# Attention on one Trainium2 core: the keys of the second head pair are loaded on ScalarE's DMA queue

## The chip, the cores and the metric

The kernel runs on one core of a Trainium2 chip. The metric is the device time in microseconds (us) of one launch; lower is better. The engines of the core are TensorE (PE, with its weight loads listed as PEld), VectorE (DVE), ScalarE (ACT), GpSimd (POOL) and SyncE (SP); transfers between the device memory and the core's SBUF are carried by 16 DMA engines and are issued here from two queues, SP's (q1 in the profile) and ScalarE's (q10).

## The reference

Softmax attention without a mask, in float32, for 8 batches of 8 heads, 512 positions and 64 columns:

```python
scale = 1.0 / np.sqrt(q.shape[-1])
scores = np.einsum('bhqd,bhkd->bhqk', q, k) * scale
scores = scores - scores.max(axis=-1, keepdims=True)
attn = np.exp(scores)
attn = attn / attn.sum(axis=-1, keepdims=True)
return np.einsum('bhqk,bhkd->bhqd', attn, v).astype(np.float32)
```

q, k, v and the output are 8 x 8 x 512 x 64 values each, 8.39 MB apiece.

## The kernel before, in words

**Tiling.** The 64 heads are taken two at a time: 32 pairs, g = 0 to 31. For each pair there are three loads of 256 KB (k, q and v, two heads of 512 x 64 float32 on 128 partitions). POOL casts them to float16 (L494, L504), PE transposes k and q (L535), DVE copies the transposes out of PSUM (L548, for pair 1 in two halves at L542), and PE then forms the scores (L575), 128 keys by 512 queries for each head and block of keys. Two such blocks are one group of 128 x 1024 scores, and there are 128 groups (the last one in two halves). For 112 of them ACT takes the exponential (L579, L777); for the other 16 DVE does it by arithmetic on the bits (L599, L616 to L639). PE multiplies by the values (L680), a column of ones beside v gives the sums, DVE takes reciprocals and scales (L645, L650), and a store goes out for each head.

**Order.** Nothing is scheduled at run time. The class `Plan` simulates the kernel with fixed durations and due times and writes out one list of steps; the body issues them in that order under `tc.manual_schedule()`, so each engine runs its instructions in a fixed order and only waits for semaphores. The plan has no notion of which queue a load is on: it has one stream of transfers.

**The start, where the change is.** `first_loads()` (L718) issues pair 0's keys in two halves on ScalarE's queue (L722) and pair 0's queries in two halves on SP's (L723). Then a loop calls `load(g, name)` for pair 1's keys ("k1" below), pair 1's queries ("q1"), k2, q2, v0, k3, q3, k4, q4, k5, q5, v1 and so on, all on SP's queue at L488. The loads' completion is told on eight semaphores taken in turn, so that SP issues a load only when the one eight places before it has landed: q4's issue waits for k1's landing, k5's for q1's, and so on; SP's later issues stand behind.

`first_pair()` (L729) handles pair 0 by itself: ACT loads its activation table (L743), then casts a part of q0 (L743), and of the second halves (L745, L746); DVE and POOL cast the rest; PE transposes them (L760, L765), with some matmuls on constants between (L727), and forms pair 0's first three groups of scores (L770), whose exponentials ACT takes at L777. The fourth group of pair 0 and all later ones are at L575 and L579.

**Pair 1.** POOL casts k1 whole (L504). q1 is cast in two halves at once, by DVE (L502) and by POOL (L503), where POOL's half stands behind its cast of k1. PE transposes k1 first and then q1 (L535, eight 128 x 128 blocks), DVE copies k1's half and then q1's (L542), and the first scores of pair 1 follow at L575. Behind these casts POOL has k2, q2 and v0.

Of the kernel before, what the change touches and what calls it, by code (L numbers as in the profile page):

```python
# [407 lines left out]
def kernel(  # L408
# [7 lines left out]
    nc = tc.nc  # L416
# [50 lines left out]
    def source(src, g):  # L467
        b, h = g // ppb, 2 * (g % ppb)
        return src[b, h : h + 2].rearrange("h (p i) d -> p h i d", i=NI)

    def load_tile(g, name):
        t = lpool.tile(
            [P, 2, NI, D],
            FP32,
            tag=f"{name}32",
            name=f"{name}32_{g}",
            bufs=7,
        )
        raw.setdefault(g, {})[name] = t
        return t  # L480

    def load(g, names):
        if g >= NP:
            return
        for name in names:
            src = {"q": q, "k": k, "v": v}[name]
            t = load_tile(g, name)
            nc.sync.dma_start(out=t[:, :, :, :], in_=source(src, g))  # L488

    def cast(g, name):  # L490
        if g >= NP:
# [325 lines left out]
    with tc.manual_schedule():  # L817
        plan = Plan(groups, NP, 3)
        steps = plan.run()
        first_loads()  # L820
        for g, name in plan.first_loads:
            load(g, name)
        make_identity(nc, ident)
        for n in range(NV):
            nc.vector.memset(vps[n][:, :, :, D : D + 1], 1.0)
        first_pair()
        do = {
            "transposes": transposes,
            "scores": scores,
            "values": values,  # L830
            "load": load,
            "store": store,
            "cast": cast_behind,
            "raise": raise_,
            "copy": lambda g, b: copy(g),
            "pass": pass_,
            "last": last_values,
            "finish": finish,
            "rec": lambda u, n, b: reciprocal(u, n),
            "mul": lambda u, n, b: normalise(u, n),  # L840
        }
        for what, *args in steps:
            do[what](*args)
# [30 lines left out]
```

## Time and profile before

| | |
|---|---|
| median of 3 runs | 114.5 us (113.86, 114.7, 114.5) |
| the profiled execution | 114.31 us, of which the span of the instructions is 112.5 us |
| POOL busy | 65.2 us (58%) |
| TensorE's granted clock, mean | 0.999 |
| read from device memory, written to it | 25.17 MB, 8.39 MB |
| DMA queue q1 (SP's), q10 (ScalarE's) | 33.04 MB, 0.52 MB |

The profile is of one execution. A row of the timeline gives the start and the length in us (merged instructions with their count), the engine (with a q where it is the engine's queue that issues something), the line, the operation, out<-in, and in brackets the engine's idle time before it and what ended that. Rows of a line's instructions give the duration in ns as minimum/median/maximum and the start of the first and the last; "DMA to landing" is the time from issue to the completion of a transfer, in us. Rows by windows give, for a stretch of the span, each engine's busy time and the number of its instructions, then the granted TensorE clock, the mean busy share of the 16 DMA engines (it can pass 1, as packets overlap) and the rate in GB/s.

### The profile page before, as it was taken

How to read it: one execution, taken by the hardware profiler on the slowest of the kernel's cores; microseconds unless marked ns; L12 is line 12 of the kernel's file. 1: busy time of each engine (PE TensorE's matmuls, PEld its weight loads, DVE VectorE, ACT ScalarE, POOL GpSimd, SP SyncE). 2: the span in 40 equal slices, each digit the busy share in tenths (PEclk: the TensorE clock that was granted, in tenths of full speed). 3: DMA queues.
4: the chain of work that ended last, by engine and by line, in shares of the span. 5: the costliest groups of instructions: out<-in, count | busy, mean ns of one | idle time of the engine just before them, and what ended most of it. 6: DMA issues, size and time to landing. Idle time of an engine off the chain costs nothing.

```text
span 112.5 us, 4427 instructions
## 1 busy us (share of the span) xinstructions
PE 104.0 (92%) x1731; PEld 71.1 (63%) x1731; DVE 101.3 (90%) x226; ACT 105.6 (94%) x118; POOL 65.2 (58%) x127
## 2 busy tenths in 40 slices
PE   7988889899999998999999999999999999999970
PEld 7654546576775564657677557678667765776560
DVE  1547999999989999999999999999999999999760
ACT  4689999999999999999999999999999999999960
POOL 2166788265478866686847888755868796000000
PEclk9999999999999999999999999999999999999999
DMA  2999999999999999999999999999997976848435
GB/s 90 271 340 354 346 349 349 342 349 348 348 329 331 344 350 347 344 353 325 283 299 376 346 312 363 358 374 353 357 305 229 289 244 212 270 143 268 159 99 184
DMA packets 35349, 33.84 MB, mean 301 GB/s; under 512 B 2560, under 2 KB 35328, under 8 KB 35328
## 3 DMA queue, kind: packets, MB, share of 16 engines
q1 hardware_dynamic: 34752, 33.04, 90.8%
q10 hardware_dynamic: 576, 0.52, 1.4%
q8 instruction: 13, 0.21, 0.8%
q14 instruction: 8, 0.07, 0.2%
HBM read 25.17 MB, written 8.39 MB: 298 GB/s over the span
## 4 chain that ended last, share of the span: by engine, by line
DVE 45%; PE 42%; ACT 7%; issue 2%; DMA 1%
PE o L680 18%; PE st L575 14%; DVE pd L599 10%; DVE tqk L548 8%; DVE ring L650 8%; ACT pt L579 7%; PE tp L535 6%; DVE m L633 4%; DVE pd L639 3%; PE st_0a L727 3%; DVE pe L625 3%; DVE m L616 2%; DVE m L635 2%; DVE rc L645 2%; DMA out_dram<-ring 1%
## 5 line engine op out<-in xcount | busy, mean ns | idle before, releaser
L579 ACT ACTIVATE pt<-st 128x1024 f16<-128x1024 f32 (+1 forms) x110 | 100.3, 1114 | 0.0
L680 PEld LDWEIGHTS <-pt 128*128 128x128 f16 x880 | 38.9, 98 | 12.3 <-issue 10.6
L680 PE MATMUL o<-vp,pt 128*128 128x65 f16 x880 | 46.3, 194 | 0.2
L575 PE MATMUL st<-tqk 64*128 64x512 f16 (+1 forms) x250 | 42.4, 381 | 2.9 <-ACT pt L579 1.7
L504 POOL CAST qkp<-k 128x512 f16<-128x512 f32 x31 | 21.5, 692 | 12.2 <-DMA k<-in_k_dram 5.2
L494 POOL CAST vp<-v 128x512 f16<-128x512 f32 x32 | 21.8, 695 | 7.7 <-DVE rc L645 2.6
L504 POOL CAST qkp<-q 128x512 f16<-128x512 f32 x30 | 21.1, 703 | 6.6 <-DVE rc L645 2.2
L650 DVE TENSOR_TENSOR ring<-o,rc 128x448 f32<-128x448 f32 (+2 forms) x37 | 22.3, 606 | 0.6
L680 PE MATMUL o<-vp,pe 128*128 128x65 f16 x128 | 22.1, 195 | 0.0
L680 PE MATMUL o<-vp,pd 128*128 128x65 f16 x128 | 21.9, 193 | 0.0
L548 DVE COPY tqk<-tp 128x1024 f16<-128x1024 f16 x30 | 20.3, 677 | 0.2 <-PE tp L535 0.2
L535 PE MATMUL tp<-ident,qkp 128*128 128x128 f16 x248 | 19.5, 219 | 0.9 <-DVE ring L650 0.7
L599 DVE TENSOR_SCALAR pd<-st 128x1024 uint16<-128x1024 f32 x16 | 19.5, 1217 | 0.7 <-PE st L575 0.7
L575 PEld LDWEIGHTS <-tqk 64*128 64x128 f16 x250 | 11.7, 93 | 12.3 <-issue 4.8
L535 PEld LDWEIGHTS <-qkp 128*128 128x128 f16 x248 | 14.3, 97 | 7.3 <-issue 4.4
L680 PEld LDWEIGHTS <-pe 128*128 128x128 f16 x128 | 12.5, 97 | 3.8 <-issue 2.9
L680 PEld LDWEIGHTS <-pd 128*128 128x128 f16 x128 | 12.5, 98 | 0.0
L639 DVE TENSOR_TENSOR pd<-pd,m 128x1024 f16<-128x1024 f16 x16 | 10.9, 682 | 0.0
L633 DVE TENSOR_TENSOR m<-m 128x1024 f16<-128x1024 f16 x16 | 10.9, 681 | 0.0
L645 DVE RECIPROCAL rc<-o 128x7 f32<-128x7 f32 (+2 forms) x37 | 7.2, 195 | 1.9 <-PE o L680 1.9
L625 DVE TENSOR_SCALAR pe<-pd 128x1024 uint16<-128x1024 uint16 x16 | 6.8, 425 | 0.0
L635 DVE TENSOR_SCALAR m<-m 128x1024 f16<-128x1024 f16 x16 | 6.5, 409 | 0.0
(50 smaller groups left out, 36.6 us busy)
## 6 DMA issues: line engine op xcount, KB each, us to landing
v<-in_v_dram SPq DMA_DIRECT2D x32, 256.0 KB, 5.8
k<-in_k_dram SPq DMA_DIRECT2D x31, 256.0 KB, 5.9
q<-in_q_dram SPq DMA_DIRECT2D x31, 256.0 KB, 5.9
out_dram<-ring SPq DMA_DIRECT2D x57, 128.0 KB, 3.7
out_dram<-ring SPq DMA_DIRECT2D x2, 256.0 KB, 3.3
k<-in_k_dram ACTq DMA_DIRECT2D x2, 128.0 KB, 2.9
q<-in_q_dram SPq DMA_DIRECT2D x2, 128.0 KB, 2.7
out_dram<-ring ACTq DMA_DIRECT2D x2, 128.0 KB, 2.0
```

What stands on the lines that cost most here:

```text
L494: return nc.gpsimd.tensor_copy(out=vps[g % NV][:, :, :, 0:D], in_=raw[g]["v"][:, :, :, :])
L504: return nc.gpsimd.tensor_copy(out=dst, in_=src[:, :, :, :])
L535: reads[g] = nc.tensor.transpose(tps[g][:, n, i, :], qkp[g][:, n, i, :], ident)
L548: nc.vector.tensor_copy(out=tqk[g][:, :, :], in_=tps.pop(g).rearrange("p n i c -> p n (i c)"))
L575: nc.tensor.matmul(st[:, x, cols], kc, qc[:, cols], start=True, stop=True)
L579: nc.scalar.activation(out=pt[:, :, cols], in_=st[:, :, cols], func=EXP, scale=scale, bias=SHIFT)
L599: nc.vector.tensor_scalar(out=r["pd"][:, :, :], in0=r["st"][:, :, :], scalar1=BITS, scalar2=BIAS, op0=AluOp.mult, op1=AluOp.add,)
L625: ins = nc.vector.tensor_scalar(out=r["pe"][:, :, :], in0=u[:, :, :], scalar1=0x7C00, scalar2=None, op0=AluOp.bitwise_and,)
L633: ins = nc.vector.tensor_tensor(out=m16, in0=m16, in1=m16, op=AluOp.mult)
L639: ins = nc.vector.tensor_tensor(out=u16, in0=u16, in1=m16, op=AluOp.mult)
L650: nc.vector.tensor_tensor(out=ring[:, u % NU : u % NU + n, :], in0=o[:, x : x + n, 0:D], in1=rcs.pop(u)[:, 0:n].broadcast_to([P, n, D]), o ...
L680: nc.tensor.matmul(os[u // 7][:, u % 7, :], part[:, y * P : (y + 1) * P], vps[g % NV][:, h, c, :], start=(n == 0), stop=(n == len(parts) - 1),
```

## The change

One transfer changes queue. The load of pair 1's keys is issued by ScalarE instead of SyncE; it stands behind the two halves of pair 0's keys on ScalarE's queue, and ahead of ScalarE's table load, because `first_loads()` and this loop come before `first_pair()`. Each of SP's later loads moves up by one place. The order of every engine's other instructions is the same, and so are the semaphores that the loads use. All lines behind L488 move down by one.

```diff
         for name in names:
             src = {"q": q, "k": k, "v": v}[name]
             t = load_tile(g, name)
-            nc.sync.dma_start(out=t[:, :, :, :], in_=source(src, g))
+            queue = nc.scalar if (g, name) == (1, "k") else nc.sync
+            queue.dma_start(out=t[:, :, :, :], in_=source(src, g))
```

## The prediction

> **What bounds the kernel now.** I read the page first, for who is busy and what ended last, then the busy time by windows, then the timeline of the first 10 us, where the moved transfer is, then the landings of the transfers around it.
>
> ```profile
> DVE 45%; PE 42%; ACT 7%; issue 2%; DMA 1%
> ...
> L579 ACT ACTIVATE pt<-st 128x1024 f16<-128x1024 f32 (+1 forms) x110 | 100.3, 1114 | 0.0
> ```
>
> The chain that ended last runs through DVE and PE; DMA has 1% of it. But the 110 exponentials of L579 have no idle time before them at all. By windows:
>
> ```profile
> core 0: us, PE busy (x) PEld busy (x) DVE busy (x) ACT busy (x) POOL busy (x), PEclk, DMA share, GB/s
> 0.00:9.43 9.43, 7.76 (x95) 5.68 (x95) 3.60 (x24) 6.40 (x10) 3.58 (x12) 1.00 0.79 247
> 9.43:26.00 16.57, 15.23 (x231) 9.72 (x230) 16.53 (x32) 16.57 (x19) 11.17 (x20) 1.00 1.09 347
> 26.00:50.00 24.00, 22.52 (x377) 15.42 (x376) 23.38 (x47) 24.00 (x27) 17.18 (x37) 1.00 1.08 343
> 50.00:90.00 40.00, 39.63 (x703) 27.38 (x700) 39.59 (x85) 40.00 (x45) 28.85 (x54) 1.00 1.00 327
> ```
>
> From 9.43 to 90 us ACT is busy 80.57 of 80.57 us and DVE 79.50. These two are full, so a delay of the moment at which they become full is paid to the end, and time saved elsewhere is worth nothing unless they become full sooner. The DMA engines are full too (share 1.00 to 1.09), but only POOL waits for them, and POOL has 28.85 busy of 40. So the change is decided in the first 9.43 us:
>
> ```profile
> 0.74 0.89 ACTq L722 DMA_DIRECT2D k<-in_k_dram  x2
> 0.75 0.86 SPq L723 DMA_DIRECT2D q<-in_q_dram  x2
> 1.66 0.43 SPq L488 DMA_DIRECT2D k<-in_k_dram  x1
> 1.67 1.28 ACT L743 ACT_TABLE_LOAD   x1 [1.67 <-PEq L858]
> 2.12 0.47 SPq L488 DMA_DIRECT2D q<-in_q_dram  x1
> ...
> 3.28 0.41 ACT L743 CAST q<-q 128x256 f16<-128x256 f32 x1 [0.33 <-DMA q<-in_q_dram]
> ...
> 4.04 0.42 PE L765 MATMUL st<-ident,q 128*128 128x128 f16 x2
> ...
> 6.13 0.61 POOL L504 CAST qkp<-k 128x512 f16<-128x512 f32 x1 [2.27 <-DMA k<-in_k_dram]
> ...
> 7.01 0.29 DVE L502 CAST qkp<-q 128x256 f16<-128x256 f32 x1
> 7.04 0.52 POOL L503 CAST qkp<-q 128x256 f16<-128x256 f32 x1 [0.29 <-DMA q<-in_q_dram]
> ...
> 7.54 0.62 PE L535 MATMUL tp<-ident,qkp 128*128 128x128 f16 x8
> 7.79 0.61 POOL L504 CAST qkp<-k 128x512 f16<-128x512 f32 x1 [0.22 <-DMA k<-in_k_dram]
> 7.97 0.76 DVE L542 COPY tqk<-tp 128x512 f16<-128x512 f16 x2 [0.67 <-PE tp L535]
> 8.35 1.94 ACT L579 ACTIVATE pt<-st 128x1024 f16<-128x1024 f32 x2
> ...
> 8.54 0.61 POOL L504 CAST qkp<-q 128x512 f16<-128x512 f32 x1
> 8.79 1.03 PE L575 MATMUL st<-tqk 64*128 64x512 f16 x6 [0.63 <-DVE tqk L542]
> 9.43 1.23 DVE L599 TENSOR_SCALAR pd<-st 128x1024 uint16<-128x1024 f32 x1 [0.71 <-PE st L575]
> ```
>
> The reader is to follow pair 1. k1 is cast at 6.13 and q1 at 7.01 to 7.04, each as it lands. Transposes run from 7.54, the two copies from 7.97, the first scores start at 8.79, and DVE's first exponential, which needs the next ones, at 9.43; from there DVE is full. ACT's two exponentials from 8.35 take 1.94 us, some 0.97 each, so the second, the first of pair 1, starts at about 9.3. Nothing between 7.54 and 9.43 waits for more than its predecessor.
>
> **ScalarE's queue.** One more issue stands ahead of the table load. Those on this queue took 0.89 for two, so 0.45 each: the table load goes from 1.67 to about 2.12 and ends at 3.40, not 2.95. The cast behind it waited for q0 until 3.28; it now starts at about 3.42, 0.14 later, and ends at 3.83. PE reads it at 4.04, behind other transposes. That slack of 0.35 (4.04 less 3.28 + 0.41) hides the 0.14: cost nothing. An issue can take longer:
>
> ```profile
> L488 SPq DMA_DIRECT2D k<-in_k_dram x31: 367/368/1184, 1.7 to 76.4; - x31
> ```
>
> At 1.18, the longest, the cast would end 0.87 later than now, and 0.5 would reach PE. That is the upper bound, and it can't be a gain; I take nothing, as the two issues on this very queue are the nearest rows. The last three casts of pair 0 on ACT and DVE wait for transfers already ahead of k1.
>
> **SP's queue.** k1's 0.43 goes, and q1, k2, q2 and so on are issued about 0.47 sooner. That is worth nothing by itself if their landing is not set by the issue, and it isn't: q1 is issued at 2.12 and cast 4.9 us later. q4, the eighth load behind k1, waits for k1's landing, and all later loads stand behind it on SP. With k1 landing 1 us later, six transfers (k2 to k4) are still queued, at some 0.75 each (POOL's casts of k2 and q2 start at 7.79 and 8.54) 4.5 us of work, so the DMA engines do not run dry.
>
> **When k1 lands** is the term that counts. Landings from the issue:
>
> ```profile
> L722 ACTq DMA_DIRECT2D k<-in_k_dram x2: 403/432/460, 0.7 to 1.2; - x2
> DMA to landing us min/median/max: 2.7/2.9/3.2
> ...
> L723 SPq DMA_DIRECT2D q<-in_q_dram x2: 381/399/417, 0.7 to 1.2; - x2
> DMA to landing us min/median/max: 2.5/2.7/2.9
> ...
> L488 SPq DMA_DIRECT2D k<-in_k_dram x1: 427/427/427, 1.7 to 1.7; - x1
> DMA to landing us min/median/max: 4.4/4.4/4.4
> ...
> L488 SPq DMA_DIRECT2D q<-in_q_dram x1: 469/469/469, 2.1 to 2.1; - x1
> DMA to landing us min/median/max: 4.9/4.9/4.9
> ```
>
> k1 lands at 1.66 + 4.4 = 6.1 and q1 at 2.12 + 4.9 = 7.0. On one queue k1 goes first and q1 second. On two, both are issued at about 1.65 and are carried side by side, as pair 0's halves are now: those on ScalarE's queue, issued at the same moments as SP's, land 0.2 to 0.3 later. If both together need as long as now, q1 lands at about 7.0 and k1 at 7.0 to 7.25. **k1 loses its place, and q1 gains none.** By the row, k1 lands at 7.25. The Trainium skill, "DMA: Bandwidth & Descriptors", section "Queues, rings and completion order", says that each DMA engine takes turns between the queues that have work, a packet at a time; by that both finish together, k1 at 7.0, and the sum below would be +0.30 in place of +0.55. Pair 0's rows agree roughly, with the lag of 0.2 to 0.3 on top.
>
> **The sum.** POOL starts k1's cast some 0.05 behind its landing (6.13 against 6.1): at 7.30 it ends at 7.91. Its half of q1 stands behind and takes 0.52, to 8.43 (now 7.56). PE then starts q1's transposes some 0.05 later (as the first scores, 8.79, follow the copies' end, 8.73), at 8.48; now copies start 0.43 behind the first transposes (7.54 to 7.97), so q1's copy starts at 8.91, takes half of 0.76, and ends at 9.29, where it now ends at 8.73. The first scores go from 8.79 to 9.35: +0.55. With a landing at 7.0 everything is 0.25 sooner, +0.30. ACT has little cover: its pair 1 exponential starts at 9.3 and the scores for it, two of the six matmuls of 1.03, are there at about 9.15, so ACT loses 0.15 to 0.40, and DVE, which starts L599 0.64 behind the first scores, all of it. I take +0.45, between the two landings: 114.31 + 0.45 = 114.76 for an execution like the profiled one. This lies 0.19 below the median of the runs shown (114.5), so against that 114.95, and I say 114.9. Behind it, POOL's casts of k2, q2 and v0 come 0.6 later; pair 2's are not needed before its transposes, and v0's only after those, which shift with the rest.
>
> **Rivals.** *Hidden.* k1 has room: POOL starts q1's half at 7.04, so k1's cast may start at 6.43 unseen, and PE takes k1's four blocks first (half of 0.62), so about 0.3 more is free: a landing up to 6.7 costs nothing. It would take place if two queues carried more than one. For it speaks a hole:
>
> ```profile
> 3.00:3.50 0.50, 0.50 (x14) 0.50 (x11) 0.22 (x2) 0.22 (x1) 0.01 (x1) 1.00 1.04 363
> 3.50:4.00 0.50, 0.50 (x9) 0.39 (x7) 0.21 (x2) 0.19 (x1) 0.36 (x1) 1.00 0.77 174
> 4.00:4.50 0.50, 0.50 (x8) 0.50 (x6) 0.43 (x3) 0.39 (x2) 0.00 (x0) 1.00 0.63 217
> 4.50:5.00 0.50, 0.50 (x7) 0.27 (x7) 0.50 (x3) 0.32 (x2) 0.00 (x0) 1.00 0.94 234
> ```
>
> With both queues at work the rate is 363 GB/s, and just as only SP's is left it falls to 174 to 234, though k1 and q1 have long been issued. Filled to 350 for these 1.5 us, the hole holds 0.21 MB, 0.6 us: both would land by 6.4. Then PE is late next (it starts the transposes behind pair 0's scores, not behind a cast), and at most 0.1 is gained: 114.2 to 114.3 on the profile's scale, 114.4 beside the median. Against it: the engines idle with work issued, so something ahead of them is slow, and a second queue need not help. The same skill page, section "Issuing engines are not separate DMA queues", says that a second issuing engine saves only the time of the issue; by that too the time stays, 114.5.
>
> *Slower by more.* The same hole read the other way: what prepares the packets of issued transfers is behind, and serves k1, newly on the other queue, behind the k2 and q2 that SP has lined up. k2 now lands just before 7.79 and q2 by 8.54. The cast of k1 would start at 7.79 or 8.54, against 7.30 in my sum, so the scores come 0.55 + 0.49 = 1.04 or 0.55 + 1.24 = 1.79 later: 115.35 to 116.1, beside the median 115.5 to 116.3. It passes 1% once k1 lands later than about 7.85, behind k2. Against it: k0's second half, on ScalarE's queue, landed at 1.18 + 3.2 = 4.4, ahead of k1, which SP issued right behind it; nobody was served out of turn there.
>
> *Faster.* For 1% DVE's first exponential would have to start over 1.1 us sooner, and pair 0's own chain does not allow that. What remains is that loads arriving 0.5 us sooner let POOL's casts fall more kindly between DVE's; no row shows a price, I put it at 113.0. That the change does not do what it says is excluded by ScalarE's instruction order, where the issue stands ahead of the table load.
>
> **The numbers.** About 1% is what a measurement of this kernel can tell from no change: below 113.35 is faster, above 115.65 slower. My forecast, k1 landing beside q1, has 0.42, with its own range 114.5 to 115.8; 0.08 of that is the slow end, where the longer issue on ACT adds its 0.5. k1 behind k2 or q2 has 0.32, hidden 0.14, faster 0.12. So faster 0.12, within 0.34 + 0.14 = 0.48, slower 0.08 + 0.32 = 0.40. The range runs from 113.9, which takes in the hidden case with the lowest run shown (113.86), to 116.4, just above k1 behind q2; about 0.12 below and 0.06 above are left out.
>
> **What would show it.** After the change the cast of k1 (6.13 now) should start at 7.0 to 7.3, directly behind its DMA, POOL's half of q1 right behind it at about 7.9, the first scores of pair 1 at 9.1 to 9.35 and DVE's first exponential at 9.7 to 10.0; ACT should show an idle time of 0.15 to 0.4 before an L580 exponential and none later. The table load should end at about 3.4 and PE's transposes stay at 4.04. I am wrong if k1 lands before 6.7, if it lands after 7.8, if the 4.04 moves, or if the delay of the first scores is not found again at the end.

## The result, and the profile after

| | before | after |
|---|---|---|
| median of 22 runs each | 114.19 us | 115.02 us |
| ratio, 95% interval | | 1.0063 [1.0046, 1.008] |
| profiled execution, its span | 114.31, 112.5 us | 114.72, 112.9 us |

The change costs 0.63%, that is 0.72 us (0.53 to 0.91), below the 1% named in the prediction and clear of zero. A few executions take longer at a lower granted clock (after: 116.2 and 116.44 us at 0.985, the others at 0.991 or more); the medians include them and the ratio does not, so it is not the quotient of the medians. From the page of the kernel after, the chain by engine, and the group of the exponentials (busy, mean ns of one | idle before, and what ended it):

```profile
DVE 44%; PE 37%; ACT 7%; DMA 6%; issue 2%; ACTq 1%; POOL 1%
...
L580 ACT ACTIVATE pt<-st 128x1024 f16<-128x1024 f32 (+1 forms) x110 | 100.4, 1111 | 1.0 <-PE st L576 1.0
```

In this execution the load of k1 is on the chain (5% of it, of DMA's 6%), and the exponentials have 1.0 us of idle time, 0.96 of it before one of them. These two shares alone are no proof: further executions of the kernel before, shown below, have DMA at 7% and 9% of the chain, through a load of v, and up to 0.6 us of idle time. The timeline of the kernel after shows where the idle time comes from (lines are one higher than before):

```profile
1.66 0.43 SPq L489 DMA_DIRECT2D q<-in_q_dram  x1
1.66 0.46 ACTq L489 DMA_DIRECT2D k<-in_k_dram  x1
...
2.15 1.28 ACT L744 ACT_TABLE_LOAD   x1 [2.15 <-issue]
...
3.44 0.41 ACT L744 CAST q<-q 128x256 f16<-128x256 f32 x1
...
4.08 0.27 PE L766 MATMUL st<-ident,q 128*128 128x128 f16 x2
...
7.16 0.29 DVE L503 CAST qkp<-q 128x256 f16<-128x256 f32 x1 [0.85 <-DMA q<-in_q_dram]
...
7.93 0.40 POOL L504 CAST qkp<-q 128x256 f16<-128x256 f32 x1
...
8.04 0.63 PE L536 MATMUL tp<-ident,qkp 128*128 128x128 f16 x8 [1.07 <-POOL qkp L505]
...
9.72 2.85 ACT L580 ACTIVATE pt<-st 128x1024 f16<-128x1024 f32 x3 [0.96 <-PE st L576]
```

k1 and q1 are issued at the same moment. q1 lands just before 7.16, about where it landed before (7.0). The chain of waits of the kernel after, in order of time (start, us, what), gives the rest without a gap:

```profile
1.66 5.65 DMA k<-in_k_dram
7.32 0.05 issue
7.37 0.62 POOL qkp L505
7.99 0.05 issue
8.04 0.41 PE tp L536 x4
8.45 0.02 issue
8.47 0.77 DVE tqk L543 x2
9.24 0.05 issue
9.29 0.62 PE st L576 x4
9.91 0.02 issue
9.93 1.23 DVE pd L600
```

k1 lands at 7.32 in place of 6.1. POOL, PE, DVE and PE follow one after the other, each within 0.05 us, and DVE's first exponential starts at 9.93 in place of 9.43. Behind that nothing has changed, as the busy times by windows show (PE, PEld, DVE, ACT, POOL; granted clock; DMA share; GB/s):

```profile
26.00:50.00 24.00, 22.55 (x371) 15.34 (x370) 23.39 (x47) 24.00 (x27) 17.18 (x39) 1.00 1.08 343
50.00:90.00 40.00, 39.63 (x710) 27.62 (x706) 39.59 (x86) 40.00 (x45) 28.85 (x53) 1.00 1.01 331
```

ACT is full again and DVE's busy times agree with before to 0.01 us. From the start of DVE's first exponential to the end of the span there were 112.5 - 9.43 = 103.1 us before and 112.9 - 9.93 = 103.0 after.

### The profile page after: what moved, and what is told of

It is laid out like the page before. It is cut to its first block, busy times and chain, and to the rows that moved or that the text cites. A ratio compares the mean times of both kernels' runs of the same rounds, so it can differ in the third digit from the quotient of the medians.

```text
span 112.9 us, 4427 instructions
## 1 busy us (share of the span) xinstructions
PE 103.0 (91%) x1731; PEld 70.4 (62%) x1731; DVE 101.2 (90%) x226; ACT 105.6 (93%) x118; POOL 65.1 (58%) x127
## 4 chain that ended last, share of the span: by engine, by line
DVE 44%; PE 37%; ACT 7%; DMA 6%; issue 2%; ACTq 1%; POOL 1%
PE o L681 18%; PE st L576 14%; DVE pd L600 10%; DVE tqk L549 8%; DVE ring L651 8%; ACT pt L580 7%; PE tp L536 6%; DMA k<-in_k_dram 5%; DVE m L634 4%; DVE pd L640 3%; DVE pe L626 3%; DVE m L617 2%; DVE m L636 2%; DVE rc L646 2%; DMA out_dram<-ring 1%
```

## The experiments

The theory is "lost place": on one queue k1 was carried first and q1 second; on two they are carried together, so k1 lands where q1 did, and q1 gains nothing. Its rivals are the longer issue on ScalarE ahead of the table load, the stream of later loads that waits for k1's landing, and a queue of ScalarE's that is slow as such. Ratios are to the kernel before, run on the same chip.

### More profiles of the two kernels

No edit; two more executions of the kernel before and one of the kernel after.

> The kernel before once more, for a second profile. In the first one PE's transposes of 128 x 128 took about 0.31 each until 6.3 us and pair 0's chain was slow; in the changed kernel's they were at 0.22 from 4 us on. If that is chance of the run and not of the change, it differs between executions of one kernel. With PE fast early the first scores of pair 1 come at 8.4 to 8.6, with PE slow at 8.8; the span is 103.1 us more than the start of DVE's first exponential, 0.65 behind those scores.

> As r1_before, a third profile of the kernel before: first scores of pair 1 at 8.4 to 8.6 where PE is fast early, at 8.8 where it is slow.

> The changed kernel once more. Theory 'lost place': k1 lands beside q1 at 7.0 to 7.4 whether PE is fast or slow early, and the first scores of pair 1 follow 1.97 us behind its landing, at 9.0 to 9.4; the span is 103.0 more than DVE's first exponential. The rival 'held stream' or any later cost: that distance grows.

The timelines, first those of the kernel before (r1, span 112.8; r2, span 112.1):

```profile
5.38 0.40 PE L765 MATMUL tp_qb<-ident,q 128*128 128x128 f16 x4
...
6.88 0.61 POOL L504 CAST qkp<-k 128x512 f16<-128x512 f32 x1 [2.93 <-DMA k<-in_k_dram]
...
9.01 0.82 PE L575 MATMUL st<-tqk 64*128 64x512 f16 x6 [0.52 <-DVE tqk L542]
...
9.66 1.23 DVE L599 TENSOR_SCALAR pd<-st 128x1024 uint16<-128x1024 f32 x1 [0.71 <-PE st L575]
```

```profile
5.08 0.40 PE L765 MATMUL tp_qb<-ident,q 128*128 128x128 f16 x4
...
6.18 0.61 POOL L504 CAST qkp<-k 128x512 f16<-128x512 f32 x1 [2.35 <-DMA k<-in_k_dram]
...
8.29 0.82 PE L575 MATMUL st<-tqk 64*128 64x512 f16 x6 [0.52 <-DVE tqk L542]
...
8.94 1.23 DVE L599 TENSOR_SCALAR pd<-st 128x1024 uint16<-128x1024 f32 x1 [0.70 <-PE st L575]
```

And of the kernel after (r3, span 113.1):

```profile
7.52 0.61 POOL L505 CAST qkp<-k 128x512 f16<-128x512 f32 x1 [3.53 <-DMA k<-in_k_dram]
...
9.44 0.82 PE L576 MATMUL st<-tqk 64*128 64x512 f16 x6 [0.62 <-DVE tqk L543]
...
10.09 1.23 DVE L600 TENSOR_SCALAR pd<-st 128x1024 uint16<-128x1024 f32 x1 [0.71 <-PE st L576]
```

One profile does not stand for the kernel here. Before, k1's cast starts at 6.13, 6.88 and 6.18 and the first scores at 8.79, 9.01 and 8.29, on average 8.70; after, at 7.37 and 7.52, and the scores at 9.29 and 9.44, on average 9.37. That is a difference of 0.67, against the 0.72 of the runs, and in all five the span ends 103.0 to 103.2 behind DVE's first exponential. What held pair 1 back before differs: in the first profile it is PE, which comes late from pair 0's scores and not from k1; in r1 and r2 PE's transposes start as the cast of k1 ends. The page of r1 shows a second limit just as late (chain by engine):

```profile
DVE 42%; PE 37%; DMA 7%; ACT 7%; SPq 2%; issue 2%; POOL 1%
```

There, and in r2, the chain that ended last runs through the load of v0, which lands at 9.80 (r2: 9.09), and not through k1. So in the kernel before an earlier k1 alone could win little. In both profiles of the kernel after the chain runs through k1's load. My expectation that a fast PE brings 8.4 to 8.6 missed on both sides: r1 has it fast, but k1 lands late there, and r2 is faster than that. r3's landing (7.47) and scores (9.44) lie just above what I expected, 7.0 to 7.4 and 9.0 to 9.4. The rival of a held stream of loads finds nothing: q4's issue moves from 6.09 to 7.33, behind k1's landing, but no time is lost behind 10 us.

### Only the order, ScalarE's queue untouched

```diff
-        for g, name in plan.first_loads:
+        early = plan.first_loads
+        for g, name in [early[1], early[0], *early[2:]]:
             load(g, name)
```

> Everything stays on SP's queue, only pair 1's queries are issued ahead of its keys. Theory 'lost place' (the changed kernel is slower because k1 now lands where q1 did, at 7.3, and POOL's cast, the transposes, the copies and the first scores of pair 1 follow one after the other): q1 lands at about 6.1 and k1 at about 7.0; k1's cast starts at 7.05 and the first scores of pair 1 about 1.9 us behind it, near 9.0, against 9.29 in the changed kernel; ratio to before 1.003 to 1.005. Rival 'ScalarE's issue' (the 0.46 us of issue ahead of ScalarE's table load is what costs): ratio 1.000, since ScalarE's queue is as before. Rival 'held stream' (the load of q4 waits for k1's landing and with it all later loads): here q4 waits for q1 instead, which lands early, so ratio 1.000.

Ratio 1.0023 [1.0, 1.0046]. In its profiled execution:

```profile
6.74 0.61 POOL L504 CAST qkp<-k 128x512 f16<-128x512 f32 x1 [3.09 <-DMA k<-in_k_dram]
...
8.68 1.03 PE L575 MATMUL st<-tqk 64*128 64x512 f16 x6 [0.58 <-DVE tqk L542]
```

k1 is cast at 6.74, 0.34 later than the mean of the three before (6.40) and 0.7 earlier than after. The loss by the ratio, about 0.26 us, lies between too, but its interval touches 1, and in this execution the first scores are no later than the mean before. The scores did not wait for k1 here: PE was slow in this execution and came from pair 0's scores only at 7.43, when k1's cast had ended. So this one is inconclusive on the price of order alone, and what I expected was missed: 7.05 for k1's cast, 9.0 for the scores, a ratio of 1.003 to 1.005. Nor does one execution show that second place on one queue is better than a place beside q1 on two: before, q1 in second place landed at 6.9 to 7.6.

### Only the issue

```diff
+        spare = cpool.tile([16, NI, D], FP32, name="spare")
+        nc.scalar.dma_start(out=spare[:, :, :], in_=source(k, 0)[0:16, 0])
         for g, name in plan.first_loads:
             load(g, name)
```

> As before, with one more transfer of 16 KB into an unused tile, issued third on ScalarE's queue. Its data are a sixteenth of k1's, its issue costs the same. Theory 'lost place': the table load ends at 3.4 instead of 2.95, the cast behind it at 3.85, still ahead of PE's need at 4.04; k1 lands at 6.1 to 6.2 as before; ratio 1.000, within 0.002. Rival 'ScalarE's issue': the full loss, ratio 1.006.

Ratio 1.0006 [0.9989, 1.0022]. Its timeline has the later table load, and PE unmoved:

```profile
2.15 1.28 ACT L743 ACT_TABLE_LOAD   x1 [2.15 <-issue]
...
3.44 0.41 ACT L743 CAST q<-q 128x256 f16<-128x256 f32 x1
...
3.99 0.42 PE L765 MATMUL st<-ident,q 128*128 128x128 f16 x2
```

The table load moves from 1.67 to 2.15 as in the kernel after, PE's transposes do not move, and nothing can be measured. The rival of ScalarE's issue falls. In this execution, the slowest of the twelve (114.78 us), k1 was cast at 6.94 and not at 6.1 to 6.2 as I expected; r1 has it at 6.88 without any edit.

### A shorter way from k1's landing to the scores

The kernel after, with its cast of k1 shared between DVE and POOL:

```diff
+        if (g, name) == (1, "k"):
+            nc.vector.tensor_copy(out=dst[:, :, 0:2], in_=src[:, :, 0:2])
+            return nc.gpsimd.tensor_copy(out=dst[:, :, 2:4], in_=src[:, :, 2:4])
         return nc.gpsimd.tensor_copy(out=dst, in_=src[:, :, :, :])
```

> The changed kernel, with its cast of k1 split between DVE and POOL (half each) as q1's already is. Nothing of the transfers changes. Theory 'lost place': k1 lands at about 7.3 as in the changed kernel, but POOL's cast of it takes 0.36 in place of 0.61, so the first scores of pair 1 come at about 9.0 in place of 9.29 and a third of the loss is won back: ratio to before 1.003 to 1.005. Rival 'held stream' or any cost that does not run through POOL's cast: ratio 1.006 as in the changed kernel.

```profile
7.29 0.29 DVE L506 CAST qkp<-k 128x256 f16<-128x256 f32 x1 [0.99 <-DMA k<-in_k_dram]
7.32 0.52 POOL L507 CAST qkp<-k 128x256 f16<-128x256 f32 x1 [3.50 <-DMA k<-in_k_dram]
7.50 0.49 DVE L503 CAST qkp<-q 128x256 f16<-128x256 f32 x1
7.64 0.94 PE L539 MATMUL tp<-ident,qkp 128*128 128x128 f16 x8 [0.67 <-DVE qkp L506]
...
9.11 0.82 PE L579 MATMUL st<-tqk 64*128 64x512 f16 x6 [0.52 <-DVE tqk L546]
```

Ratio 1.0031 [1.0009, 1.0052]. k1 lands as late as in the kernel after, at 7.3, but the first scores come 1.82 us behind the start of its cast and not 1.92, and the ratio is half the loss. The point estimates go with the theory: what shortens the way from k1's landing to the scores wins time back. It is not shown clear of noise: the interval still reaches 1.005, and that of the kernel after begins at 1.0046. The profile shows less than the ratio, 0.1 of that distance: POOL's half of k1 took 0.52 and not the 0.36 I expected, so that PE's four transposes of k1 take 0.56 in place of 0.41.

### Other ways to use the two queues

Head 0 of k1 and of q1 on SP's queue, head 1 of both on ScalarE's (e3); only k1 so, and both heads of q1 in two transfers on SP's (e6); k1 and q1 in two transfers each, all on SP's (e7); only k1 in two, one for each queue, and q1 whole (e9). For e3:

```diff
+        for g, name in plan.first_loads[:2]:
+            t, src = load_tile(g, name), source({"q": q, "k": k}[name], g)
+            nc.sync.dma_start(out=t[:, 0], in_=src[:, 0])
+            nc.scalar.dma_start(out=t[:, 1], in_=src[:, 1])
-        for g, name in plan.first_loads:
+        for g, name in plan.first_loads[2:]:
             load(g, name)
```

> Both queues are used for pair 1, but the order k1 ahead of q1 is kept on each: head 0 of k1 and then head 0 of q1 on SP's queue, head 1 of each on ScalarE's. Theory 'lost place': both halves of k1 land together at about 6.2 and q1's at about 7.1, so that the first scores come as before or up to 0.2 later, from the two issues ahead of the table load (it ends at 3.9 and the cast behind it at 4.3, 0.25 behind PE's need); ratio 1.000 to 1.002. Rival 'a second queue is slow as such': the half on ScalarE's queue lands at 7 or later and the ratio is 1.005 or more. Rival 'two queues fill the hole between 3.5 and 5.0 us': the rate there is near 350 GB/s in place of 200, q1 has landed by 6.5, ratio below 1.

> Head 0 of k1 first on SP's queue, head 1 of k1 third on ScalarE's, then both heads of q1 in two transfers on SP's: one more issue on ScalarE, as in the changed kernel, but nothing of q1 ahead of k1. Theory 'lost place': k1 lands at 5.5 to 6.2 and q1 by 7.0; no loss, ratio 0.998 to 1.001, and below 1 if smaller transfers fill the hole at 3.5 to 5.0 and q1 lands before 6.6. Rival 'any use of ScalarE's queue for pair 1 costs': 1.003 or more.

> All on SP's queue, k1 and q1 in two transfers each, in the old order. It tells why the rate is low between 3.5 and 5.0 us in the kernel before. Theory 'the first 256 KB transfer is slow to be prepared': with transfers of 128 KB the rate there is near 300 GB/s or more, k1 lands by 5.6 and q1 by 6.5, ratio 0.998 to 1.000. Rival 'one queue alone is slow at that moment': the rate stays near 200, k1 at 6.1, q1 at 7.0; ratio 1.000 to 1.002 with the two more issues.

> Head 0 of k1 first on SP's queue, head 1 third on ScalarE's, and everything else whole on SP's queue as before. One more transfer in all, so q2 is held until k0's first half has landed, at 3.4, and v0 comes 0.3 later than before, not 0.6 as with two more. Theory 'lost place': k1 lands at 5.5 to 6.2, q1 at 6.7 to 7.0; first scores at 8.4 to 8.8 and no loss; ratio 0.997 to 1.002. It would beat both kernels if q1 gains 0.3 and v0 is not late. Rival 'ScalarE's queue costs': 1.004 or more.

| | ratio, 95% interval | k1's cast at | first scores at |
|---|---|---|---|
| e3 | 1.0028 [1.0007, 1.0049] | 5.50 | 8.63 |
| e6 | 1.0042 [1.0016, 1.0067] | 6.09 | 8.61 |
| e7 | 1.0045 [1.0023, 1.0066] | 5.69 | 8.76 |
| e9 | 1.0012 [0.9983, 1.004] | 6.39 | 8.97 |

The two columns on the right are of one execution each; e9's took 115.78 us, 1.2 above the median of its runs, and stands for little.

With the order kept, half of k1 on ScalarE's queue is not slow: in e3 and e6 k1 is cast at 5.50 and 6.09, and pair 1's first scores are as early as before. So the queue is not slow as such. Nor does an earlier k1 win anything: in e3, where q1 is early too (cast at 6.10 and 6.71), PE comes from pair 0's scores only at 7.38.

Three of them lose, by another way than the kernel after: e7 does not touch ScalarE's queue for pair 1 at all. In e6:

```profile
9.85 0.62 POOL L494 CAST vp<-v 128x512 f16<-128x512 f32 x1 [0.28 <-DMA v<-in_v_dram]
...
10.52 0.41 PE L680 MATMUL o<-vp,pt 128*128 128x65 f16 x8 [0.33 <-POOL vp L494]
...
11.52 0.18 DVE L645 RECIPROCAL rc<-o 128x3 f32<-128x3 f32 x1 [0.45 <-PE o L680]
```

Each further transfer takes one of the eight semaphores, so k2 or q2 is held until a half of pair 0 has landed (k2 is issued at 3.55 in e6, at 2.64 before), and v0 comes late for these scores: POOL casts it at 9.85 (in the first profile before, 9.29), PE waits 0.33 for it, and DVE, full by then, 0.45 for PE. The end then comes 113.1 - 9.26 = 103.8 behind DVE's first exponential, not 103.1. In e7 it is the same (v0's cast at 9.91, DVE waits 0.36). That the held issue is what makes v0 late is argued, not shown: r1, with no further transfer, casts it at 9.85 too, but there DVE's first exponential starts at 9.66 and DVE does not wait.

e3 goes another way: its v0 is cast at 9.53, and PE takes it up at 10.20 as in the first profile before; its chain starts with the two further issues on ScalarE, behind which the table load ends at 3.92 and PE's transposes stand at 4.39, not 4.04. Whether that is its 0.28% stays open. My expectations for e6 (0.998 to 1.001) and e7 (0.998 to 1.000) missed this; e3 lies above its 1.000 to 1.002, which its interval still covers.

The low rate between 3.5 and 5.0 us was higher in e3 (windows; the last column is GB/s):

```profile
3.50:4.00 0.50, 0.50 (x9) 0.37 (x5) 0.08 (x2) 0.49 (x2) 0.19 (x1) 1.00 0.96 285
4.00:4.50 0.50, 0.25 (x4) 0.12 (x3) 0.39 (x2) 0.50 (x2) 0.00 (x0) 1.00 0.96 326
4.50:5.00 0.50, 0.50 (x5) 0.33 (x4) 0.18 (x1) 0.45 (x2) 0.00 (x0) 1.00 1.10 375
```

e7, with the same sizes on SP's queue alone, has 258, 184 and 332 there, between the two answers expected, so why the rate is low is not settled.

No version beats the kernel before; e9 is equal to it within its interval.

### Two that remain partly open

v0 in place of k1 on ScalarE's queue (e4), and both k1 and q1 on it (e8):

```diff
-            nc.sync.dma_start(out=t[:, :, :, :], in_=source(src, g))
+            queue = nc.scalar if (g, name) == (0, "v") else nc.sync
+            queue.dma_start(out=t[:, :, :, :], in_=source(src, g))
```

(and v0 taken first in the loop, so that it is issued beside k1; e8 names (1, "k") and (1, "q") there instead, in the old order)

> k1 and q1 are first on SP's queue as before; instead a load that nobody needs before 9.3 us, pair 0's values, goes third on ScalarE's queue. Theory 'lost place by sharing' (a transfer on ScalarE's queue takes half of the rate from what SP has in line): k1 lands at about 7.1 beside v0, q1 at about 7.9; the first scores of pair 1 at 9.2 to 9.4, as late as in the changed kernel; ratio 1.005 to 1.008, although neither k1 nor q1 has changed queue. Rival 'ScalarE's queue is slow for its own transfers only': k1 at 6.1, q1 at 7.0, ratio 1.000.

> A larger dose: k1 and q1 both go whole to ScalarE's queue, so k2 and q2 are first on SP's. Theory 'lost place by sharing': k1 lands beside k2 at about 7.1 and q1 beside q2 at about 8.6; POOL's half of q1 ends near 9.1 and the first scores of pair 1 come near 10, 0.7 later than in the changed kernel; with the second issue ahead of the table load ratio 1.011 to 1.014. Rival 'the queues are served in the order of issue': k1 and q1 at 6.5 to 7.3, ratio 1.006 or less.

e4: ratio 1.0037 [1.0013, 1.006], between the two theories. Its profiled execution, at 114.08 us the fastest of its runs, does not show the loss:

```profile
6.42 0.61 POOL L505 CAST qkp<-k 128x512 f16<-128x512 f32 x1 [2.71 <-DMA k<-in_k_dram]
...
7.25 0.52 POOL L504 CAST qkp<-q 128x256 f16<-128x256 f32 x1 [0.22 <-DMA q<-in_q_dram]
...
8.64 0.96 PE L576 MATMUL st<-tqk 64*128 64x512 f16 x6 [0.52 <-DVE tqk L543]
```

k1 comes at 6.42 and q1 at 7.25, neither by my numbers (7.1 and 7.9), and the scores at 8.64 are as early as before. e8: the recorded ratio is 1.018 [1.0121, 1.0239], more than expected. But its six runs fall into two groups, 114.97, 115.45 and 115.57 us, and 116.94 to 117.3 us; the first group alone is 0.9% above the kernel before, between the rival's 1.006 and the theory's 1.011, and three runs are few. In its profile, the fastest run of its kernel (114.97), q1 is what is late:

```profile
6.67 0.61 POOL L505 CAST qkp<-k 128x512 f16<-128x512 f32 x1 [2.59 <-DMA k<-in_k_dram]
...
8.13 0.52 POOL L504 CAST qkp<-q 128x256 f16<-128x256 f32 x1 [0.84 <-DMA q<-in_q_dram]
...
9.51 0.82 PE L576 MATMUL st<-tqk 64*128 64x512 f16 x6 [0.52 <-DVE tqk L543]
```

The scores are 0.8 later than the mean before (8.70), 0.7% of the time, most of the 0.9%.

What both show, though the times I expected were 0.5 to 0.7 too late, is the pairing. Issued at the same moment on the two queues, k1 and v0 land at 6.4 and 6.6 in e4, k2 and k1 at 6.5 and 6.6 in e8, and there q2 and q1 at 7.9 and 8.1 behind them (issue plus "DMA to landing"). In the kernel after it was q1 and k1, at 7.1 and 7.3, and in r3 7.3 and 7.5. In all five pairs the two are 0.1 to 0.2 apart, the one on ScalarE's queue last. In a row on SP's queue, two such transfers landed 0.7 to 1.0 apart (6.1 and 7.0, 6.8 and 7.6, 6.1 and 6.9 before; 5.8 and 6.7 in e1). Why the pair is there by 6.6 in e4 and e8 and only at 7.3 to 7.5 in the kernel after stays open.

## Why the prediction was right

**The bound.** It rested on ACT and DVE being full from 9.43 us, so that a delay of their start is paid to the end. That is the best supported step: in all five profiles of the two kernels the end comes 103.0 to 103.2 us behind DVE's first exponential.

**When k1 lands.** Forecast 7.0 to 7.25; 7.32 and 7.47 measured. The row of pair 0's halves, in which ScalarE's queue lagged by 0.2 to 0.3, was the better guide, though the lag was about 0.2 this time (k1 cast at 7.37 and 7.52, q1 at 7.16 and 7.29). Turns packet by packet, as the Trainium skill has them ("DMA: Bandwidth & Descriptors", "Queues, rings and completion order"), would have them finish together; the traces agree with that to 0.2 us.

**From there to the scores.** Forecast 9.35, measured 9.29 and 9.44; the first is so near because k1 was cast 0.07 later than forecast and one link was shorter. That link is POOL's half of q1: it took 0.40, not 0.52, and was done at 8.33, so that PE's second four transposes did not wait for it. The chain runs through k1's cast alone.

**ScalarE's issue.** The table load ends at 3.43 (forecast 3.40), the cast behind it at 3.85, PE's transposes moved from 4.04 to 4.08 (4.17 in r3). The prediction named a move of the 4.04 as a sign of being wrong; it lies within the scatter of the kernel before, which has 4.13 and 3.95 in r1 and r2, and e2 puts the price at zero within 0.2%.

**The sum.** This is the term that was mis-sized, +0.45 for a measured 0.72 (0.53 to 0.91). Two things made it small. I put it between the two landings, 7.0 and 7.25, and k1 landed behind the later one, for which the sum was +0.55. And the profile before was taken as the kernel's mean: its first scores at 8.79 are 0.09 later than the mean of three. With both put right the sum is 0.64, inside the measured interval. That the forecast of 114.9 us lies so near the 115.02 is luck: the three runs it started from have a median of 114.5, 0.31 above that of the 22, which makes up for the 0.27 that the step lacks. ACT's idle time was foretold at 0.15 to 0.4 and was 0.96, and 0.71 in r3: pair 0's exponentials came earlier in these executions, as PE was fast sooner, and ACT waited longer for scores that were as late as foretold. Part of that idle time belongs to the execution and not to the change: r1, of the kernel before, has 0.57.

**The rivals.** Hidden would have needed a landing by 6.7, and k1 landed 0.6 later. Behind k2 it did not land: k2, behind q1 on SP's queue, lands at about 7.9 (2.13 + 5.8), 0.6 later than k1. Faster had no mechanism, and none appeared. The hole at 3.5 to 5.0 us, on which both sides rested, was not filled by moving one transfer of 256 KB: the kernel after has 168, 180 and 170 GB/s there.

## What to carry to other kernels

Two whole transfers that are needed one after the other were better issued one after the other on one queue: there the first landed 0.7 to 1.0 us ahead of the second, and on two queues they landed within 0.2, the first as late as the second. Ask of a moved load not when it is issued but what it will be carried beside, and price it by the way from its landing to the first work of the engine that is full. And where one event starts the full stretch, look for it in several profiled executions before a difference of half a microsecond is read from two.

## What the runs showed of the hardware that was not expected

**PE's first matmuls.** In the first profile before, a single 128 x 128 transpose at 6.1 us still took 314 ns; in the kernel after, one of the same shape took 223 ns at 3.9 us. By lines, before and then after:

```profile
L760 PE MATMUL tp_kb<-ident,k x2: 314/314/314, 6.1 to 6.2; 128*128 128x128 f16 x2
```

```profile
L761 PE MATMUL st_ka<-ident,k x1: 223/223/223, 3.9 to 3.9; 128*128 128x128 f16 x1
```

It is the execution and not the change: in r2 of the kernel before PE is fast early too (four transposes in 0.40 us at 5.08, against 0.61 at 5.67 in the first), and in r3 of the kernel after the one at 4.0 us is slow (315 ns). The granted clock of the profile is 1.00 in all these windows, so it does not tell the two apart. The Trainium skill, "TensorE: Matmul & The Clock Gate", "Part 1: The HAM clock gate (the "warmup" mystery)", says that the array runs at half rate until a window of 3.4 us that does not start with the kernel has been busy; the moments seen here would fit that, the durations differ by 1.4 and not by two, and no run here tests it.

**The scatter of landings.** k1, first on SP's queue in three executions of one kernel, was cast at 6.13, 6.18 and 6.88. With that and with PE's speed the first scores lay between 8.29 and 9.01, 0.7 us apart, as much as the change costs.

**A low rate with work in line.** From 3.5 to 5.0 us the DMA engines moved 174 to 234 GB/s in the first profile before (127 to 311 with r1 and r2), with at least four transfers issued and not yet landed; with k1 and q1 in transfers of 128 KB on both queues, 285 to 375 (e3), and with these on SP's queue alone 184 to 332 (e7). Why was not settled.
